# One fused VectorE instruction per modulation tile, one borrowed weight tile put back into the ring, and two branch hints

## The chip, the core and the metric

The kernel runs on one NeuronCore of one Trainium2 chip. The core has a matmul engine (TensorE, PE in the profile), three engines for elementwise work (VectorE or DVE, ScalarE or ACT, GpSimd or POOL), SyncE (SP), which here issues nearly all DMAs, and 16 DMA engines. PE reads SBUF and writes PSUM; a PSUM bank holds 128x512 f32 values. Each engine works through its own list of instructions in order and meets the others at semaphores. The metric is device time in microseconds, lower is better.

## The reference

One layer of a diffusion backbone over 512 latent tokens and 256 context tokens of width 1024. The conditioning vector `c` gives six rows of modulation (shift, scale and gate for each half of the layer):

```
sh1, sc1, gt1, sh2, sc2, gt2 = split(silu(c) @ ada_w + ada_b, 6)
h   = rms_norm(x, norm1_g) * (1 + sc1) + sh1
...   one projection of h; two branches (retention, long convolution), merged by sigmoid gates, w_out -> mix
x   = x + gt1 * mix
h2  = rms_norm(x, norm2_g) * (1 + sc2) + sh2
x   = x + gt2 * moe(h2)
out = rms_norm(x, final_norm_g)
```

The mixture of experts picks one of 4 groups per token and 2 of its 8 experts; each expert is (silu(u w1) * (u w3)) w2 with a hidden width of 512. Rows 1 and 2 of the modulation (`sh1`, `sc1`) are needed at the start; the later four (`gt1`, `sh2`, `sc2`, `gt2`) only after the merge of the branches.

## The kernel before

**Order.** Up to the merge, Tile's scheduler places the instructions of each engine from the program order and priorities; `weave` interleaves a bulk stream of matmuls with side work, one step of each in turn. The start and the last stages are ordered by hand. In the expert stage PE alone is in hand order (`tensor_order`), and a `no_sync_barrier` is a line that the scheduler moves nothing across; it costs no instruction.

**The merge stage.** `fm_group` (through `stream`) multiplies a weight by activations held as pairs of a high and a low part (three matmuls, `mm3`, lines 201 to 203). A weight arrives as `raw` (two k-blocks per load, two buffers); ACT rounds the high part `wH` (line 197), DVE subtracts it for the low part `wL` (line 198), three buffers each. Four PSUM banks collect a group's result; the next group needs them back. Groups `gr` and `gh` are evacuated by ACT (sigmoid), `ho` and `ro` by DVE (lines 1121, 1125, 1126). They run in the order gr, gh, ho, ro, gr, gh, ho, ro for two halves of the channels.

**The later modulation rows.** From the first `ho` on the generator `rest_of_modulation` is woven in. `ada_sums` (line 333 on) computes two rows of the modulation at a time without PE: for each of 8 k-blocks and both rows it loads a 128x1024 tile of `ada2` (SP, line 340, into `ring`, four buffers of tag "c"), scales it by the per-partition value silu(c) on DVE (line 341), and, but for the first, adds it to `acc` on POOL (line 343). That is 32 tiles in two calls, 28 of them added. `ada_rows` sums `acc` over the partitions on PE (line 349), `to_columns` transposes the rows (line 357), `columns` adds the bias on DVE (line 361), and a small product `lc` of PE (line 1081) uses the result at once.

**The expert stage.** 16 pairs of experts, 12 weight tiles of 1 MB per pair: tiles 12a to 12a+7 for `up` (lines 1497), 12a+8 to 12a+11 for `down` (line 1522); pairs 2g and 2g+1 make group g. `ahead(n)` lets SP issue loads up to tile n in a fixed order. Most go to `ring_`, 10 buffers of 1 MB (tag "ew", line 1224). `loans` lists the tiles that borrow other buffers instead: two of every 13 borrow the four halves of `xm` (line 1206), one of every 13 the buffers xe0 and xe1. Tiles 128 to 131 are taken out of the `xm` loans, since the branch below uses `xm`.

**The overflow branch.** A pass gives each expert 64 token places. If an expert has more tokens, further rounds are needed: `overflow()`, called in group 5 (a = OV = 10), loads the number of rounds into a register of every engine, and `tc.If(rounds > 1)` (line 1560) skips or enters a loop nest that loads weights into the `xm` buffers. In the profiled run it is skipped. Ahead of it SP has issued up to tile 131 (`ahead(12 * OV + 8 + OA)`, OA = 4), and PE ends with `add(parts, places[4:])` (`co` matmuls, line 1537).

Of the kernel before, what the change touches and what calls it, by code (L numbers as in the profile page):

```python
# [15 lines left out]
ALU = mybir.AluOpType  # L16
# [12 lines left out]
GENERAL = True  # L29
OV = 10  # L30
OA = 4
NA, NB, NC, NR, NW, NH = 12, 33, 4, 10, 2, 3
# [141 lines left out]
def body(es: ExitStack, tc: tile.TileContext, d, out, dump=None):  # L174
    nc = tc.nc
    V, A, T, G, S = nc.vector, nc.scalar, nc.tensor, nc.gpsimd, nc.sync
# [13 lines left out]
    def bank(name, tag="x"):  # L190
        return ps.tile([128, 512], F32, name=name, tag=tag, bufs=4)
# [39 lines left out]
    def wide(name, shape=(128, 1024), dt=F32):  # L231
        return pa.tile(list(shape), dt, name=name, tag="a", bufs=NA)

    def ring(name, shape=(128, 1024), dt=F32):
        return pb.tile(list(shape), dt, name=name, tag="c", bufs=NC)
# [43 lines left out]
    scT = sm.tile([128, 8, 32], F32, name="scT")  # L279
# [54 lines left out]
    def ada_sums(r, acc):  # L334
        for k in range(8):
            for i in range(2):
                if k == 0:
                    acc.append(wide("acc"))
                w = ring("adaw")
                tc.keep_in_program_order(S.dma_start(w, d["ada2"][2 * r - 2 + i, :, k, :]))  # L340
                V.tensor_scalar(out=w if k else acc[i], in0=w, scalar1=scT[:, k, 0:1], scalar2=None, op0=ALU.mult)
                if k:
                    G.tensor_tensor(out=acc[i], in0=acc[i], in1=w, op=ALU.add)  # L343
                yield

    def ada_rows(acc, rows):
# [834 lines left out]
    def borrow(pool, tag, bufs, units):  # L1181
        def tile_():
            w = pool().tile([128, units, 512], F32, name="xw" + tag, tag=tag, bufs=bufs)
            return [w[:, u] for u in range(units)], w.rearrange("p a b -> p (a b)")
        return tile_
# [6 lines left out]
    early_tiles = len(sequence)  # L1192
    sequence += range(early_tiles, len(plan))

    loans.update((i, lent_xm) for i in range(early_tiles, len(plan) - 4)
                 if (i - early_tiles) % (NR + 3) < 2 and not 12 * OV + 8 <= i < 12 * OV + 8 + OA)
    loans.update((i, [borrow(wk_, "xe0", 1, 2), borrow(lambda: late, "xe1", 1, 2)]) for i in range(early_tiles, len(plan) - 4)
                 if (i - early_tiles) % (NR + 3) == XE)
    ready, lent = {}, {}
# [2 lines left out]
    def borrowed(src, places):  # L1202
        units = []
        for u, w in places:
            c0 = 512 * len(units)
            S.dma_start(w, src(slice(c0, c0 + 512 * len(u))))
            units += u
        return units

    def ahead(n):  # L1210

        while issued[0] < min(n, len(plan)):
            i = sequence[issued[0]]
            src = plan[i]
            issued[0] += 1
            if i in loans:
                if i < early_tiles and not lent:

                    lent.update((j, [place() for place in loans[j]]) for j in AL)
                ready[i] = borrowed(lambda c: src[:, c], lent.pop(i, None) or [place() for place in loans[i]])  # L1220
                continue
            w = ring_.tile([128, 2048], F32, name="ew", tag="ew")
            if i < len(plan) - 4:
                S.dma_start(w, src)  # L1224
            else:
                wv = w.rearrange("p (a b) -> p a b", a=4)
                for h in ((0, 4),) if i < len(plan) - 1 else ((0, 2), (2, 4)):
                    S.dma_start(wv[:, h[0]:h[1]], src[:, h[0]:h[1]])
            ready[i] = [w[:, 512 * u:512 * u + 512] for u in range(4)]
# [166 lines left out]
    for t in range(1, 4):  # L1396
# [6 lines left out]
                           op0=ALU.add, op1=ALU.mult)  # L1403
# [102 lines left out]
    def turned(hh):  # L1506
        p = bank("hT")
        for q in range(4):
            T.transpose(p[:, 128 * q:128 * q + 128], hh[:, 128 * q:128 * q + 128], ident)  # L1509
        hT_ = wk.tile([128, 512], F32, name="hT", tag="hT", bufs=2)  # L1510
        V.tensor_copy(hT_, p)
        return hT_
# [27 lines left out]
    def add(parts, places):  # L1540
        for t, n in places:
            ns = slice(512 * n, 512 * n + 512)
            p = bank("co")
            combine(parts, t, n, p, True)
            V.tensor_tensor(out=xmid[:, t, ns], in0=xmid[:, t, ns], in1=p, op=ALU.add)  # L1545
# [10 lines left out]
    def overflow():  # L1556
        later = wk.tile([128, CAP], F32, name="later")
        V.tensor_copy(later, slots)
        rounds = nc.values_load(nrounds[0:1, 0:1], min_val=0, max_val=8)
        with tc.If(rounds > 1):  # L1560
            with tc.For_i(1, rounds, 1):
                V.tensor_scalar(out=later, in0=later, scalar1=float(CAP), scalar2=None, op0=ALU.add)
                with tc.For_i(0, 16, 1) as pi:
                    pos2 = wk.tile([128, 4, 2], F32, name="pos2", tag="fs")
                    V.tensor_copy(pos2, pos[:, :, bass.ds(pi * 2, 2)])
                    whl2 = wk.tile([128, 4, 4], F32R, name="whl2", tag="whl2")
                    V.tensor_copy(whl2, f(wHL[:, :, bass.ds(pi, 1)].rearrange("p t a h e -> p t (a h e)")))
                    sel = []
                    run(select_steps(pos2, 2, "x", sel, later, "y", 4))
                    gt, xg = sel  # L1570

                    def weights(stage, kc, i, e):
                        t_, k1 = (d["w2"], 1) if stage else (d[("w1", "w3")[i]], 2)
                        return borrowed(lambda c: t_[bass.ds(pi * 2 + e, 1), :, 2 * k1 * kc + k1 * c.start // 1024:
                                                     2 * k1 * kc + k1 * c.stop // 1024, :]
                                        .rearrange("o p a b -> p (o a b)"), [place() for place in lent_xm])

                    cmb, wsl = spread(gt, 0, whl2)
                    ab_ = [bank("ga", "acc"), bank("up", "acc")]
                    for kc in range(2):  # L1580
                        up_half(ab_, kc, xg, 0, weights)
                    add([(cmb, down(turned(hidden(ab_)), wsl, weights))], places)
# [12 lines left out]
    more = chosen(0, sel)  # L1595
# [31 lines left out]
    parts = []  # L1627
    for g in range(8):
        a = 2 * g
        ahead(early_tiles + XE if g == 0 else 12 * OV + 8 + OA if a == OV else 12 * a + early_tiles + 14)  # L1630
        if g == 0:
            ab_ = [bank("ga", "acc"), bank("up", "acc")]
            up_half(ab_, 0, sel[1], 0, ahead_weights)
            run(more)
            shares()
            t1e.close()
            late = es.enter_context(tc.tile_pool(name="late", bufs=1, side="right", reuse_waits="tile"))
            ahead(early_tiles + 14)
            up_half(ab_, 1, sel[1], 0, ahead_weights)
            hh = hidden(ab_)  # L1640
            spr = [spread(sel[0], 128 * j, weights_of(j)) for j in range(2)]
            hT_ = turned(hh)
        else:
            hh = up(a, sel[1])
            add(parts, places[:4])
            hT_ = turned(hh)
            add(parts, places[4:])
        parts = []
        if a == OV and GENERAL:
            region.__exit__(None, None, None)  # L1650
            tc.no_sync_barrier()
            overflow()
            region = tensor_order()
            region.__enter__()
        ahead(12 * a + early_tiles + 20)
        now, nxt = spr, []
        parts.append((now[0][0], down(hT_, now[0][1], ahead_weights)))
        more = chosen(g + 1, nxt) if g < 7 else iter(())
        some(more, 1)
        if g == 7:  # L1660
            fn = wk.tile([128, 1024], F32, name="fn", tag="gt", bufs=1)
            for j in range(2):
                row = wk.tile([1, 512], F32, name="fr%d" % j, tag="cmb", bufs=4)
                S.dma_start(row, d["fnorm"][:, 512 * j:512 * j + 512])
                G.partition_broadcast(fn[:, 512 * j:512 * j + 512], row)
        hh = up(a + 1, sel[1])
        if g < 7:
            some(more, 3)
            hT_ = turned(hh)
            run(more)  # L1670
            spr = [spread(nxt[0], 128 * j, weights_of(a + 2 + j)) for j in range(2)]
            parts.append((now[1][0], down(hT_, now[1][1], ahead_weights)))
            sel = nxt
# [74 lines left out]
    with tc.manual_schedule():  # L1748
        ys_ = [bank("y", "acc"), bank("y", "x")]
        w = [[ahead_weights(1, n, 0, e) for e in range(2)] for n in range(2)]  # L1750
# [43 lines left out]
```

## Time and profile before

| | |
|---|---|
| median of 3 runs | 1158.91 us (1158.83 to 1163.09) |
| the profiled execution | 1160.5 us, its span 1158.5 us |
| PE busy in the span | 1109.2 us |
| DVE busy | 616.3 us |
| ACT busy | 349.8 us |
| POOL busy | 92.8 us |
| DMA moved | 283.22 MB, 244 GB/s over the span |

Times in the profile count from the start of the span. In its rows, the engine stands before the line of the kernel, the operation and the tiles (written <- read), then shapes and the count. `x4 | 5.1, 1284 | 0.3 <- ...` means four instructions, busy 5.1 us, 1284 ns each on the mean, and 0.3 us in which the engine stood idle before them, with what ended the idle time. `A <- B: 6.2, 1, 6.2` in the view of waits: A waited for B 6.2 us in total, once, 6.2 us at the longest. A `q` behind an engine (SPq, PEq) is its sequencer: waits, branches, DMA issues. PE's rows overlap, as matmuls are pipelined; the step from one start to the next is the better measure.

### The profile page before, as it was taken

How to read it: one execution, taken by the hardware profiler on the slowest of the kernel's cores; microseconds unless marked ns; L12 is line 12 of the kernel's file. 1: busy time of each engine (PE TensorE's matmuls, PEld its weight loads, DVE VectorE, ACT ScalarE, POOL GpSimd, SP SyncE). 2: the span in 40 equal slices, each digit the busy share in tenths (PEclk: the TensorE clock that was granted, in tenths of full speed). 3: DMA queues.
4: the chain of work that ended last, by engine and by line, in shares of the span. 5: the costliest groups of instructions: out<-in, count | busy, mean ns of one | idle time of the engine just before them, and what ended most of it. 6: DMA issues, size and time to landing. Idle time of an engine off the chain costs nothing. (4 is left out here: it accounts for less than half of the span.)

```text
span 1158.5 us, 13777 instructions
## 1 busy us (share of the span) xinstructions
PE 1109.2 (96%) x5338; PEld 714.9 (62%) x5338; DVE 616.3 (53%) x1041; ACT 349.8 (30%) x620; POOL 92.8 (8%) x69
## 2 busy tenths in 40 slices
PE   6999999999999997779999999999999999899996
PEld 3667888877778776558775735454545454444543
DVE  1778996675466759988543623333333333232234
ACT  2486352445444463223243411020202020101112
POOL 0010000000000005676000000000000000000000
PEclk8999999999999998889999999999999999999998
DMA  7653343121222045565384888999999994999992
GB/s 263 196 176 102 113 142 125 55 73 55 73 73 73 19 156 192 179 218 182 109 332 195 320 324 345 417 419 418 415 417 416 419 416 173 418 418 417 418 406 102
DMA packets 63279, 283.22 MB, mean 244 GB/s; under 512 B 6822, under 2 KB 8998, under 8 KB 44778
## 3 DMA queue, kind: packets, MB, share of 16 engines
q1 hardware_dynamic: 61114, 274.51, 62.2%
q0 software_dynamic: 2096, 7.80, 2.1%
q8 instruction: 43, 0.70, 0.2%
q14 instruction: 26, 0.21, 0.0%
HBM read 280.18 MB, written 2.10 MB: 244 GB/s over the span
## 5 line engine op out<-in xcount | busy, mean ns | idle before, releaser
L198 DVE TENSOR_TENSOR wL<-raw,wH 128x512 fp32r<-128x512 f32 x142 | 131.3, 931 | 118.1 <-ACT wH L197 110.0
L197 ACT CAST wH<-raw 128x512 fp32r<-128x512 f32 x142 | 88.1, 621 | 232.0 <-PE ro L202 34.9
L1497 PE MATMUL ga<-ew,xgm 128*64 128x512 f32 x408 | 110.3, 593 | 2.2 <-DMA ew<-w 2.2
L1503 DVE TENSOR_TENSOR hh<-hh,up 128x512 f32<-128x512 f32 x16 | 11.0, 688 | 184.5 <-PE up L1497 184.5
L1497 PE MATMUL up<-ew,xgm 128*64 128x512 f32 x376 | 103.3, 593 | 2.7 <-DMA ew<-w 2.7
L1522 PE MATMUL y<-ew,hT 128*64 128x512 f32 x368 | 95.9, 595 | 2.9 <-PEq L1560 1.9
L343 POOL TENSOR_TENSOR acc<-acc,adaw 128x1024 f32<-128x1024 f32 x28 | 74.3, 2664 | 84.6 <-PE gh L202 43.7
L197 ACT CAST yh<-yv 128x512 fp32r<-128x512 f32 x30 | 18.5, 618 | 200.1 <-DVE yv L1528 188.5
L1497 PEld LDWEIGHTS ga<-ew,xgm 128*64 128x64 f32 x408 | 34.1, 137 | 61.4 <-issue 53.7
L1497 PEld LDWEIGHTS up<-ew,xgm 128*64 128x64 f32 x376 | 32.9, 137 | 55.3 <-issue 47.6
L1465 PE MATMUL xg<-gtm,h2H 128*128 128x256 f32 x256 | 60.5, 280 | 0.0
L1466 PE MATMUL xg<-gtm,h2L 128*128 128x256 f32 x256 | 59.8, 278 | 0.0
L1522 PEld LDWEIGHTS y<-ew,hT 128*64 128x64 f32 x368 | 29.8, 137 | 48.1 <-issue 44.4
L1528 DVE SCALAR_TENSOR_TENSOR yv<-y,wsl,gt 128x512 f32<-128x512 f32 x30 | 22.4, 748 | 61.6 <-PE y L1522 53.1
L1502 ACT ACTIVATE hh<-ga 128x512 f32<-128x512 f32 x16 | 9.6, 597 | 138.2 <-PE ga L1497 135.9
L1465 PEld LDWEIGHTS xg<-gtm,h2H 128*128 128x128 f32 x256 | 48.1, 188 | 0.8 <-issue 0.8
L1466 PEld LDWEIGHTS xg<-gtm,h2L 128*128 128x128 f32 x256 | 48.1, 188 | 0.0
L1545 DVE TENSOR_TENSOR xmid<-xmid,co 128x512 f32<-128x512 f32 x58 | 39.8, 688 | 12.5 <-PE co L1537 11.9
L1537 PE MATMUL co<-yh,cmb 128*128 128x512 f32 x114 | 46.1, 404 | 0.0
L1468 DVE TENSOR_TENSOR xgm<-xg,rss 128x256 f32<-128x256 f32 x64 | 27.0, 424 | 35.3 <-PE xg L1466 35.3
L1537 PE MATMUL co<-yl,cmb 128*128 128x512 f32 x114 | 44.7, 392 | 0.0
L1469 ACT ACTIVATE xgm<-xgm,sh2c 128x256 f32<-128x256 f32 x64 | 32.4, 509 | 35.7 <-DVE xgm L1468 35.7
(479 smaller groups left out, 2437.0 us busy)
## 6 DMA issues: line engine op xcount, KB each, us to landing
ew<-w SPq DMA_DIRECT2D x147, 1024.0 KB, 13.6
xwxm<-w SPq DMA_DIRECT2D x54, 512.0 KB, 15.0
raw<-w_in SPq DMA_DIRECT2D x52, 512.0 KB, 3.7
adaw<-ada SPq DMA_DIRECT2D x32, 512.0 KB, 5.2
xwxe<-w SPq DMA_DIRECT2D x26, 512.0 KB, 17.4
adaw<-ada SPq DMA_DIRECT2D x32, 256.0 KB, 5.9
raw<-ret_w_o SPq DMA_DIRECT2D x8, 512.0 KB, 3.7
raw<-w_out SPq DMA_DIRECT2D x8, 512.0 KB, 4.0
```

The costliest lines, as they stand in the source:

```text
L197: A.copy(h, src)
L198: V.tensor_tensor(out=l, in0=src, in1=f(h), op=ALU.subtract)
L343: G.tensor_tensor(out=acc[i], in0=acc[i], in1=w, op=ALU.add)
L1465: T.matmul(p, h2[0][:, t, ks], gt[:, t], start=(t == 0), stop=False)
L1466: T.matmul(p, h2[1][:, t, ks], gt[:, t], start=False, stop=(t == 3))
L1468: V.tensor_tensor(out=x_, in0=p, in1=rss, op=ALU.mult)
L1469: A.activation(x_, x_, AF.Identity, bias=sh2c[:, k:k + 1])
L1497: T.matmul(ab_[i][64 * e:64 * e + 64], xg[k][:, c0 + 64 * e:c0 + 64 * e + 64], w[e][q], start=(k == 0), stop=(k == 7))
L1522: T.matmul(y_[n][64 * e:64 * e + 64], hT_[:, 128 * k + 64 * e:128 * k + 64 * e + 64], w[e][2 * q + n], start=(k == 0), stop=(k == 3))
L1528: V.scalar_tensor_tensor(out=yv, in0=y_[n], scalar=wsl, in1=gt2[:, ns], op0=ALU.mult, op1=ALU.mult)
L1537: T.matmul(p, cmb[:, 128 * t:128 * t + 128], y[j][:, ns], start=(start and i + j == 0), stop=(i == len(parts) - 1 and j == 1))
L1545: V.tensor_tensor(out=xmid[:, t, ns], in0=xmid[:, t, ns], in1=p, op=ALU.add)
```

## The change

Three edits. In `ada_sums` the scaling on DVE and the addition on POOL become one `scalar_tensor_tensor` on DVE (tile times scalar plus `acc`) for the 28 tiles that are added; the first tile of each sum keeps its scaling. In `loans` the range that is left out of the `xm` loans grows by 8 tiles, from 128..131 to 128..139; a tile in it that was to borrow `xm` uses the ring. The branch gets a label, and two hint instructions (`LikelyTaken`) for it are placed: on SP ahead of the loads of tiles 128 to 131, and on PE between the two halves of the `co` matmuls ahead of the branch, each between two scheduling barriers.

```
@@ ada_sums
-                V.tensor_scalar(out=w if k else acc[i], in0=w, scalar1=scT[:, k, 0:1], scalar2=None, op0=ALU.mult)
                 if k:
-                    G.tensor_tensor(out=acc[i], in0=acc[i], in1=w, op=ALU.add)
+                    V.scalar_tensor_tensor(out=acc[i], in0=w, scalar=scT[:, k, 0:1], in1=acc[i], op0=ALU.mult, op1=ALU.add)
+                else:
+                    V.tensor_scalar(out=acc[i], in0=w, scalar1=scT[:, k, 0:1], scalar2=None, op0=ALU.mult)
@@ loans
-                 if (i - early_tiles) % (NR + 3) < 2 and not 12 * OV + 8 <= i < 12 * OV + 8 + OA)
+                 if (i - early_tiles) % (NR + 3) < 2 and not 12 * OV + 8 <= i < 12 * OV + 8 + OA + 8)
@@ overflow
-        with tc.If(rounds > 1):
+        with tc.If(rounds > 1, label="more"):
@@ the loop over groups, a = 2 * g
+        if a == OV and GENERAL:
+            ahead(12 * OV + 8)
+            tc.no_sync_barrier()
+            tc.mark_branch_hint_location("more", hint="LikelyTaken", engines=[mybir.EngineType.SP])
+            tc.no_sync_barrier()
         ahead(early_tiles + XE if g == 0 else 12 * OV + 8 + OA if a == OV else 12 * a + early_tiles + 14)
...
             hT_ = turned(hh)
+            if a == OV and GENERAL:
+                tc.no_sync_barrier()
+                tc.mark_branch_hint_location("more", hint="LikelyTaken", engines=[mybir.EngineType.PE])
+                tc.no_sync_barrier()
             add(parts, places[4:])
```

Here `early_tiles` is 14, `NR` 10 and `GENERAL` true.

## The prediction

> **What bounds the kernel now.** I read the page first (busy time, slices), then the waits of PE, then the stretches in which PE waits, engine by engine. TensorE (PE) is busy through nearly the whole span, so time can come only from the few places where it waits or runs slowly.
>
> ```profile
> PE 1109.2 (96%) x5338; PEld 714.9 (62%) x5338; DVE 616.3 (53%) x1041; ACT 349.8 (30%) x620; POOL 92.8 (8%) x69
> ...
> PEclk8999999999999998889999999999999999999998
> ```
>
> The granted clock dips in slices 15 to 17 of 40 (434 to 521 us). This is the merge stage, where the later modulation rows are summed between matmuls. The waits of PE from 433.5 to 576.2 us, and the stretches in which the clock is halved (columns: stretch, its length, then busy us and count of PE, PEld, DVE, ACT, POOL, clock, DMA share, GB/s):
>
> ```profile
> PE lc L1081 <- DVE sh2c L361: 6.9, 1, 6.9
> PE ro L201 <- DVE sig L1121: 6.2, 1, 6.2
> PE gr L201 <- DVE sig L1125: 5.0, 1, 5.0
> PE ro L203 <- DVE wL L198: 1.0, 1, 1.0
> ```
> ```profile
> 449.00:455.84 6.84, 4.54 (x11) 3.65 (x12) 6.41 (x9) 0.00 (x0) 1.53 (x2) 0.50 0.62 210
> ...
> 479.73:486.56 6.83, 4.05 (x10) 3.22 (x11) 6.83 (x10) 1.50 (x3) 1.48 (x1) 0.50 0.67 222
> ...
> 513.87:520.69 6.82, 4.04 (x23) 3.29 (x23) 4.24 (x5) 0.00 (x0) 5.93 (x3) 0.50 0.37 139
> ```
>
> All four waits are for VectorE (DVE): 19.1 us. Behind each of the three long ones the clock is 0.50, and PE works 4.54, 4.05 and 4.04 us in that state; half of it is lost, 6.3 us. So 25.4 us hang on DVE being late. Why it is late:
>
> ```profile
> 433.50:550.00 116.50, 97.38 (x406) 75.43 (x406) 104.39 (x90) 34.13 (x56) 74.47 (x29) 0.91 0.58 194
> ```
> ```profile
> L198 DVE TENSOR_TENSOR wL<-raw,wH 128x512 fp32r<-128x512 f32 x32 | 56.1, 1766 | 6.8 <-ACT wH L197 6.8
> L341 DVE TENSOR_SCALAR adaw<-adaw,scT 128x1024 f32<-128x1024 f32 x27 | 30.5, 1149 | 2.1 <-DMA adaw<-ada 2.1
> ...
> L198 DVE TENSOR_TENSOR retL<-o,retH 128x512 fp32r<-128x512 f32 x8 | 7.6, 956 | 0.0
> ```
> ```profile
> L198 DVE TENSOR_TENSOR wL<-raw,wH x32: 677/1687/2884, 434.2 to 550.0; 128x512 fp32r<-128x512 f32 x32
> ...
> L341 DVE TENSOR_SCALAR adaw<-adaw,scT x28: 735/743/2891, 432.7 to 543.0; 128x1024 f32<-128x1024 f32 x28
> ...
> L343 POOL TENSOR_TENSOR acc<-acc,adaw x28: 2376/2713/2842, 433.6 to 546.0; 128x1024 f32<-128x1024 f32 x28
> ```
>
> DVE is busy 104.4 of 116.5 us, 90%. But the same wL instruction takes 0.68 us or 2.9, and the scaling of one tile 0.74 or 2.9. The timelines of GpSimd (POOL) and DVE show when:
>
> ```profile
> 475.72 5.50 POOL L343 TENSOR_TENSOR acc<-acc,adaw 128x1024 f32<-128x1024 f32 x2 [1.36 <-DVE adaw L341]
> ```
> ```profile
> 476.16 5.60 DVE L198 TENSOR_TENSOR wL<-raw,wH 128x512 fp32r<-128x512 f32 x2
> 481.68 1.27 DVE L1125 TENSOR_TENSOR sig<-sig,ro 128x512 f32<-128x512 f32 x2
> ```
>
> Two wL that lie inside two POOL additions last as long as these (5.60 against 5.50 us). L1125, for whose PSUM bank PE waits 5.0 us, stands behind them. Much of what is counted as DVE work here is waiting for POOL.
>
> The second place is the overflow branch at 960 to 1100 us. Its rows: the first `co` matmul of the expert groups 4 to 7, then what line 1560 (the branch) did, then the issues of SP, then the DMA rate in 2 us slices from 930 us.
>
> ```profile
> 907.79 0.50 PE L1537 MATMUL co<-yh,cmb 128*128 128x512 f32 x1
> ...
> 967.84 0.50 PE L1537 MATMUL co<-yh,cmb 128*128 128x512 f32 x1
> ...
> 1035.21 0.50 PE L1537 MATMUL co<-yh,cmb 128*128 128x512 f32 x1
> ...
> 1097.85 0.50 PE L1537 MATMUL co<-yh,cmb 128*128 128x512 f32 x1
> ```
> ```profile
> L1560 SPq EVENT_SEMAPHORE  x8: 17/17/17, 965.2 to 965.8; - x8
> ...
> L1560 SPq COMPARE_BRANCH  x1: 50/50/50, 958.6 to 958.6; - x1
> ...
> L1560 PEldq COMPARE_BRANCH  x1: 3618/3618/3618, 973.8 to 973.8; - x1
> ```
> ```profile
> 937.48 20.48 SPq L1224 DMA_DIRECT2D ew<-w  x5
> 977.51 0.87 SPq L1206 DMA_DIRECT2D xwxm<-w  x2
> 978.43 3.64 SPq L1224 DMA_DIRECT2D ew<-w  x6
> ```
> ```profile
> GB/s 404 434 408 422 418 414 430 422 408 412 426 430 401 422 389 414 164 16 0 0 0 0 8 4 174 365 354 418 410 442 414 426 410 414 412 420 438 410 422 408
> ```
>
> A group of four experts takes 60.05 us up to the branch (967.84 - 907.79), then 67.37, then 62.64: 7.32 + 2.59 = 9.9 us over. SP issues nothing from 958 to 977.5, so the DMA engines run dry at 964 and are at full rate again after 980. The load of tile 132 (`xwxm`) stands first, and six ring loads follow it at once: they had only stood behind it.
>
> ```profile
> SPq L1206 <- PEq L1560: 11.3, 1, 11.3
> ```
> ```profile
> 977.76 7.09 PE L1522 MATMUL y<-ew,hT 128*64 128x512 f32 x32 [1.86 <-PEq L1560]
> ```
>
> SP waited 11.3 us there for PE's passing of the branch, and PE itself lost 1.9 us at it (the bracket of its next row).
>
> **The modulation sums.** Removed: 28 scalings on DVE (27 of them in the row: 30.5 us) and 28 additions on POOL (2.71 us each, about 74 us). Added: 28 scalar_tensor_tensor of 128x1024 with two SBUF sources on DVE. The trace has none of that width. Nearest rows:
>
> ```profile
> L517 DVE SCALAR_TENSOR_TENSOR cv<-up,pp,cv x24: 743/746/751, 78.2 to 152.3; 128x511 f32<-128x511 f32 x24
> ```
> ```profile
> L411 DVE SCALAR_TENSOR_TENSOR fsd<-win,l x8: 1131/1151/1173, 74.5 to 93.3; 128x512 f32<-128x512 f32 x8
> ```
> ```profile
> L1545 DVE TENSOR_TENSOR xmid<-xmid,co 128x512 f32<-128x512 f32 x58 | 39.8, 688 | 12.5 <-PE co L1537 11.9
> L1468 DVE TENSOR_TENSOR xgm<-xg,rss 128x256 f32<-128x256 f32 x64 | 27.0, 424 | 35.3 <-PE xg L1466 35.3
> ```
>
> 256 more columns cost 0.264 us, so L517's 0.746 becomes 0.746 + 2 x 0.264 = 1.27 us at 1024. Lower bound: 0.74, the scaling it replaces. Upper bound: twice L411, which writes its halves interleaved, 2.30. I take 1.27, from L517, which has the same contiguous form with two SBUF sources and a per-partition scalar: 28 x (1.27 - 0.74) = 14.8 us more DVE work.
>
> With POOL quiet the stretched instructions fall to their minima: wL 56.1 - 32 x 0.68 = 34.3, retL 7.6 - 8 x 0.68 = 2.2, the scalings 30.5 - 27 x 0.74 = 10.5; together 47 us. DVE then has 104.4 - 47 + 14.8 = 72 us to do, in a stretch that would shrink by 22 us to 94: 77%. It keeps up on the whole, with little to spare at the transitions, where the evacuations of four banks and the splits come together. So I leave an estimate at each: 0.7 us at `ho` to `ro`, one wL that stands ahead; 1 us at `ro` to `gr`, one evacuation (1.27 us for two in the row of L1125) and the hand-over; 1.5 us at `lc`, where two small additions and a wL between them must pass after the transposes. That is 3.2 of 19.1 us, none long enough for the clock: it halved behind waits of 5.0 us and more and not behind 1.0. Gain: 15.9 + 6.3 = 22.2 us.
>
> The loads are an SP matter: an `adaw` buffer comes free at the end of the DVE instruction instead of POOL's, which takes away SP's waits for POOL here, and lets the next weight loads pass earlier.
>
> ```profile
> SPq L340 <- POOL acc L343: 10.5, 5, 2.8
> ```
> ```profile
> DMA to landing us min/median/max: 3.8/5.5/7.8
> ```
>
> **Tile 132 and the hints.** The longer exclusion takes in only one more borrowed tile, 132: the others of 128 to 139 are ring tiles, or 139, which another line lends. Tile 132 now takes the ring buffer of 121, 133 to 137 those of 122 to 125 and 127, 138 that of 128. PE's reading of 120 onwards:
>
> ```profile
> 954.00 3.60 PE L1497 MATMUL ga<-ew,xgm 128*64 128x512 f32 x16
> 957.44 3.60 PE L1497 MATMUL up<-ew,xgm 128*64 128x512 f32 x16
> ```
>
> Two tiles go per 3.43 us, so 132 may go at once after the branch, 133 and 134 at 961, 135 and 136 at 964.5, 137 at 968. None waits for the branch on PE. At 2.5 us per tile (1.05 MB at 418 GB/s) they keep the DMA busy to about 980, where 128 comes free. So of the dry 15 us some 2 to 3 remain (1 to 2 more if SP still stalls from 958.6 to 965.2 at its own branch). Tiles 138 and 139 land near 987; PE reads them about 993. There is 6 us to spare, and the following group, which before lost 2.6, starts with loads ahead. I cost the lost ring buffer at nothing for that reason; if the cover went, it would be one tile, 2.5 us. DMA waits gone: 9.9 - 1.9 = 8.0 us.
>
> The hint on PE, some 30 matmuls ahead of the branch, should hide the 3.6 us that the branch takes: 1.5 of PE's 1.9 us. Bounds: 0 if it does nothing, 3.6 us lost if what it fetches displaces PE's own next instructions. [...] The scheduling barriers order nothing that DVE or ACT lack time for there.
>
> **Sum.** 22.2 + 8.0 + 1.5 = 31.7 us. On the profiled execution (1160.5 us, span 1158.5) that gives 1128.8; the median of the runs is 1158.9, 1.6 lower, so I forecast 1127.
>
> **The rivals.**
> *DVE becomes the bound.* The new instruction costs 2.30 us, as L411's row would have it: 28 x (2.30 - 1.27) = 29 us more than I count, DVE 101 us where PE needs 94; these 7 us go, and some 4 more where DVE is late at the transitions (half the clock's 6.3 and 1 us of waits): 1127 + 11 = 1138. For it: L411 also has two SBUF sources. Against it: L517 has too, at 0.746. [...] 10%.
> *The ring is no release.* The wait of SP for PE's branch moves to tile 133, or the exclusion changes nothing that decides: then only the merge stage gains, 1158.9 - 22 = 1137. For it: every engine meets at line 1560. Against it: six ring loads went out in 3.64 us, unhindered. 10%.
> *Slower: the DVE queue stands behind its own loads.* A fused instruction waits for its load in order, ahead of the wL that PE needs. A load takes up to 7.8 us; POOL's slowness has given it time. It decides if each of the 16 pairs of loads holds DVE over 2.3 us beyond what the three weight buffers cover (16 x 2.3 = 37, more than all that can be won). At 3 us each: 48 - 32 = 16 us slower, 1175. Against it: DVE waited 2.1 us in all for these loads, and SP gets rid of 10.5 us of waits. 4%.
> *It does nothing that counts* (a new order of the instructions takes back what is won): 1157. 3%.
>
> **How the numbers follow.** Forecast 73%. The best case, no wait left at all, is 1158.9 - 25.4 - 9.9 = 1123.6; with the scatter of the runs I begin at 1120. The upper end takes in the two rivals that lose one of the halves, 1138, and a little more: 1141. Outside stay some 10%. Faster by over 0.5% (5.8 us, about what a measurement of this kernel can tell from no change): 73 + 10 + 10, and 1 of the rest, 0.94; same 0.02; slower 0.04.
>
> **What would show it.** In the merge stage: wL at 0.68 us throughout, the fused instruction near 1.27, clock 1.0 from 434 to 576 us, PE's waits for DVE under 4 us in all. At the branch: tile 132 issued before 966 us of today's count, no run of zeros in the DMA rate, groups of 60 us on both sides, PE's branch well under 3.6 us. A fused instruction of 2 us or more, DVE waiting for `adaw`, or SP still silent until PE has passed the branch would make it wrong.

## The result, and the profile after

| | before | after |
|---|---|---|
| median | 1161.0 us (4 runs, 1158.8 to 1164.1) | 1124.6 us (4 runs, 1124.1 to 1125.2) |
| the profiled execution, its span | 1160.5, 1158.5 us | 1124.3, 1122.6 us |

The ratio is 0.9685, 95% interval [0.9656, 0.9713]: 36.6 us less than before by this ratio. 1127.0 us was forecast. (The runs of before beside the kernel after have a median 2 us above the 1158.9 that the forecast starts from.)

The page of the kernel after: busy time and the granted clock.

```profile
PE 1100.6 (98%) x5338; PEld 710.5 (63%) x5338; DVE 582.1 (52%) x1041; ACT 349.4 (31%) x620; POOL 18.6 (2%) x41
...
PEclk8999999999999999999999999999999999999999
```

The three dips of the clock in slices 15 to 17 are gone, and POOL has 28 instructions fewer. The waits of PE from 433.5 to 1110 us are down to two:

```profile
PE y L1523 <- DVE hT L1512: 1.1, 1, 1.1
PE y L1523 <- PEq L1561: 0.5, 1, 0.5
```

The merge stage of the kernel after: the stretch of 96.5 us (busy us and count of PE, PEld, DVE, ACT, POOL, then clock, DMA share, GB/s), then the fused instruction and the split wL on DVE, and DVE's waits.

```profile
433.50:530.00 96.50, 96.50 (x432) 76.36 (x431) 72.42 (x95) 33.05 (x56) 0.18 (x1) 1.00 0.72 239
```
```profile
L342 DVE SCALAR_TENSOR_TENSOR acc<-adaw,scT,acc x28: 1277/1283/1286, 430.6 to 514.3; 128x1024 f32<-128x1024 f32 x28
```
```profile
L198 DVE TENSOR_TENSOR wL<-raw,wH x45: 682/691/693, 431.8 to 559.6; 128x512 fp32r<-128x512 f32 x45
```
```profile
DVE acc L342 <- DMA adaw<-ada: 9.9, 7, 2.1
```

PE is busy in all 96.5 us at full clock. DVE is busy 72.4 of them (75%), and every wL takes 0.69 us where it took up to 2.88. DVE now waits 9.9 us for the weight loads, which it did for 2.1 us before, but no wait of PE follows from it.

The branch after: the first `co` matmul of groups 4 to 7, then the branch (now line 1561), the two hints, and the DMA rate in 2 us slices from 900 us.

```profile
881.10 0.50 PE L1538 MATMUL co<-yh,cmb 128*128 128x512 f32 x1
...
941.14 0.50 PE L1538 MATMUL co<-yh,cmb 128*128 128x512 f32 x1
...
1002.01 0.50 PE L1538 MATMUL co<-yh,cmb 128*128 128x512 f32 x1
...
1062.04 0.50 PE L1538 MATMUL co<-yh,cmb 128*128 128x512 f32 x1
```
```profile
L1561 SPq EVENT_SEMAPHORE  x8: 17/17/17, 938.0 to 940.5; - x8
L1561 SPq COMPARE_BRANCH  x1: 70/70/70, 932.6 to 932.6; - x1
...
L1561 PEldq COMPARE_BRANCH  x1: 2341/2341/2341, 947.1 to 947.1; - x1
```
```profile
L1801 SPq BRANCH_PREFETCH_HINT  x1: 56/56/56, 924.4 to 924.4; - x1
L1801 PEldq BRANCH_PREFETCH_HINT  x1: 45/45/45, 943.1 to 943.1; - x1
```
```profile
GB/s 414 412 424 416 418 418 418 418 434 403 408 432 416 418 418 393 344 410 406 53 66 279 426 430 414 434 406 303 383 317 393 410 434 418 438 389 414 420 420 426
```

The groups take 60.04, 60.87 and 60.03 us: 0.8 us over instead of 9.9. The dry stretch of the DMA engines has shrunk to two slices. SP is still silent at its branch, though its hint came 8.2 us earlier: the branch is at 932.6, the first instruction behind it at 938.0, the next load at 940.6. PE's branch takes 2.3 us and ends 6.3 us after PE's hint.

Matched matmul by matmul, PE is 2.3 us ahead of before already at its hundredth matmul (33.3 against 31.0 us), when the first stretch at half clock was shorter in that execution (6.8 us instead of 10.2): this is no work of the change. From the first `ho` to the first `wo` matmul, 142.7 us become 116.8: 25.8 us. Then 1.6 us are given back in expert group 0, where the clock is halved behind the 1.1 us wait for hT (which the kernel before has too, at full clock):

```profile
647.38:650.79 3.41, 3.41 (x10) 0.99 (x10) 1.10 (x4) 0.00 (x0) 0.00 (x0) 0.50 0.46 186
```

At the branch 9.1 us are gained. 2.3 + 25.8 - 1.6 + 9.1 = 35.6 of the 35.9 us between the spans.

### The profile page after: what moved, and what is told of

Same layout as the page of the kernel before. It is cut to its first block, busy times and chain, and to the rows that moved or that the text cites. A ratio compares the mean times of both kernels' runs of the same rounds, so it can differ in the third digit from the quotient of the medians.

```text
span 1122.6 us, 13708 instructions
## 1 busy us (share of the span) xinstructions
PE 1100.6 (98%) x5338; PEld 710.5 (63%) x5338; DVE 582.1 (52%) x1041; ACT 349.4 (31%) x620; POOL 18.6 (2%) x41
## 5 line engine op out<-in xcount | busy, mean ns | idle before, releaser
L198 DVE TENSOR_TENSOR wL<-raw,wH 128x512 fp32r<-128x512 f32 x142 | 97.2, 688 | 120.0 <-ACT wH L197 111.3
L1498 PE MATMUL up<-ew,xgm 128*64 128x512 f32 x376 | 100.9, 592 | 0.0
L1498 PEld LDWEIGHTS up<-ew,xgm 128*64 128x64 f32 x376 | 31.9, 137 | 54.3 <-issue 52.9
L342 DVE SCALAR_TENSOR_TENSOR acc<-adaw,scT,acc 128x1024 f32<-128x1024 f32 x28 | 35.6, 1282 | 10.8 <-DMA adaw<-ada 10.7
```

The costliest lines, as they stand in the source:

```text
L198: V.tensor_tensor(out=l, in0=src, in1=f(h), op=ALU.subtract)
L342: V.scalar_tensor_tensor(out=acc[i], in0=w, scalar=scT[:, k, 0:1], in1=acc[i], op0=ALU.mult, op1=ALU.add)
L1498: T.matmul(ab_[i][64 * e:64 * e + 64], xg[k][:, c0 + 64 * e:c0 + 64 * e + 64], w[e][q], start=(k == 0), stop=(k == 7))
```

## The experiments

Two questions. In the merge stage: is it POOL's quiet that helps, as argued, or that there is one instruction instead of two? At the branch: what do the ring and the two hints do, each for itself? The theory is that of the prediction (POOL's additions stretched what DVE did at the same time; tile 132 held up the loads behind it; the hints are worth little); the rivals stand in each expectation. The median of before beside these kernels was 1161.3 to 1162.0 us.

**The fused instruction alone** (the first hunk of the diff, nothing else).

> The kernel before with the fused VectorE instruction alone; ring range and branch as before. Theory (the merge stage's delay came from POOL's additions holding up DVE, and the half clock behind it): the merge stage shortens by about 25 us as in the kernel after, PE waits for nothing in it, the branch still costs its 9 to 10 us; some 1135 us, ratio about 0.978. Rival (the ring and the hints carry the gain, the merge stage pays only in part): 1145 us or more. The new 1.1 us wait of PE in expert group 0 and the half clock behind it should be there already, if the earlier arrival at that place causes it; if the ring or the hints cause it, it is not.

Measured: 1134.8 us, ratio 0.9783 [0.9768, 0.9798], 25 us less. No wait of PE in the merge stage; first `ho` to first `wo` 116.8 us as in the kernel after. The two groups at the branch still take 8.7 us too much. So the merge stage's part stands by itself. Group 0's wait of 1.1 us is there, the half clock behind it isn't.

**The POOL load put back.**

```
                 if k:
                     V.scalar_tensor_tensor(out=acc[i], in0=w, scalar=scT[:, k, 0:1], in1=acc[i], op0=ALU.mult, op1=ALU.add)
+                    G.tensor_tensor(out=w, in0=w, in1=w, op=ALU.add)
```

> The kernel after, with one more POOL addition of 128x1024 behind each fused instruction (the tile added to itself; nothing reads the result), so that VectorE has the work of the kernel after and POOL is as busy as in the kernel before. Theory (what stretched VectorE's instructions was POOL's work at the same time): the split wL takes up to 2.9 us again, the merge stage gets back PE's waits and the half clock, 15 to 25 us slower than the kernel after, 1140 to 1150 us. Rival (the gain comes from there being fewer or shorter VectorE instructions, POOL is of no account): wL stays at 0.68 us, 1125 us, within 2 us of the kernel after.

Measured: 1152.5 us, ratio 0.9923 [0.9900, 0.9947], 28 us above the kernel after. PE's waits from 380 to 1110 us, and the longest stretch at half clock, in this kernel:

```profile
PE gr L201 <- DVE sig L1127: 6.7, 1, 6.7
PE lc L1083 <- DVE sh2c L363: 6.1, 1, 6.1
PE ro L201 <- DVE sig L1123: 5.2, 1, 5.2
PE ro L203 <- DVE wL L198: 1.1, 2, 0.7
```
```profile
475.20:485.44 10.24, 5.50 (x13) 4.37 (x14) 10.24 (x13) 1.94 (x4) 3.45 (x2) 0.50 0.59 206
```
```profile
L342 DVE SCALAR_TENSOR_TENSOR acc<-adaw,scT,acc x28: 1269/1274/2916, 429.8 to 542.4; 128x1024 f32<-128x1024 f32 x28
```

The three waits are back with their 18.0 us in the places that they had before, and the clock is halved behind each. DVE executes what it executes in the kernel after; only POOL is busy beside it (50.1 of the 96.5 us from 433.5 us on, 0.2 in the kernel after), and single instructions of 1.27 us now last 2.9. The wL take 1.38 us on the mean instead of 0.69, at most 2.4 where 2.9 was expected:

```profile
L198 DVE TENSOR_TENSOR wL<-raw,wH 128x512 fp32r<-128x512 f32 x32 | 43.9, 1381 | 8.2 <-ACT wH L197 7.8 <-PE ho L202 0.2
```

POOL also holds each `adaw` buffer longer here, but late loads are not the reason: DVE waited 2.3 us for them, against 9.9 in the kernel after. The time is 2.5 us above the range expected. The clock was halved for 27 us here, for 20.5 before, which may account for it.

**Two DVE instructions, POOL quiet.**

```
+                V.tensor_scalar(out=w if k else acc[i], in0=w, scalar1=scT[:, k, 0:1], scalar2=None, op0=ALU.mult)
                 if k:
-                    V.scalar_tensor_tensor(out=acc[i], in0=w, scalar=scT[:, k, 0:1], in1=acc[i], op0=ALU.mult, op1=ALU.add)
-                else:
-                    V.tensor_scalar(out=acc[i], in0=w, scalar1=scT[:, k, 0:1], scalar2=None, op0=ALU.mult)
+                    V.tensor_tensor(out=acc[i], in0=acc[i], in1=w, op=ALU.add)
```

> The kernel after, with the fused instruction split into two on VectorE (scale at 0.74 us, add at 1.3 to 1.4 us), POOL quiet. Theory: POOL's quiet gives most of the gain; VectorE has some 0.8 x 28 = 22 us more to do in the merge stage, 94 of 96.5 us, so it just about keeps up, with some waits of PE at the transitions: 1126 to 1136 us. Rival (the fusing itself carries the gain): 1150 us or more. Rival (VectorE has room that its busy time hides): 1125 us, no wait in the stage.

Measured: 1124.9 us, ratio 0.9675 [0.9653, 0.9696]: the time of the kernel after. Its first 96.5 us of the merge stage, and the addition:

```profile
433.50:530.00 96.50, 95.08 (x425) 74.90 (x424) 89.64 (x124) 35.85 (x59) 0.18 (x1) 1.00 0.74 248
```
```profile
L343 DVE TENSOR_TENSOR acc<-acc,adaw x28: 1207/1218/1226, 436.7 to 526.1; 128x1024 f32<-128x1024 f32 x28
```

DVE is busy 89.6 of 96.5 us (93%), and PE waits for it once, 1.4 us at `lc`. So the fusing saves 0.68 us an instruction (0.75 + 1.22 against 1.28), of which next to nothing reaches the time. What counted is that POOL adds nothing any more (busy 0.2 of the 96.5 us). More waits had been expected (1126 to 1136 us); the rival that VectorE has room that its busy time hides came nearest. DVE kept up here at 93% with every wL under 0.70 us; in the kernel before, at 90% with wL of up to 2.88 us, it did not.

**The ring alone** (the second hunk).

> The kernel before with the longer exclusion alone (tile 132 loads into a ring buffer); no hints, modulation as before. Theory (tile 132 stood at the branch and held up every load behind it): PE's waits for loads behind the branch go, its own wait at the branch (1.9 us) stays or grows a little since instruction fetch now meets full DMA traffic; 8 us less, some 1151 to 1153 us, ratio 0.993. Rival 1 (the wait only moves to tile 133): no change, 1159 to 1161. Rival 2 (it is the hints that bring the branch's gain): under 4 us less.

Measured: 1158.6 us, ratio 0.9978 [0.9965, 0.9990]: 2.6 us, a third of what was expected. The waits for loads behind the branch are all gone, as the theory has it. But PE's branch itself has become longer:

```profile
PE y L1522 <- PEq L1560: 4.8, 1, 4.8
```
```profile
L1560 PEldq COMPARE_BRANCH  x1: 6585/6585/6585, 974.3 to 974.3; - x1
```

Before, PE passed its branch in 3.6 us while the DMA rate stood at 0 to 8 GB/s. Here, with the loads running at 418 to 430 GB/s, it takes 6.6; PE waits 4.8 us instead of 1.9, and the clock is halved behind it for 6.8 us. The ring took one wait away and made the other one longer.

While PE passes its branch in the kernel before (973.8 to 977.4 us), a single DMA packet moves, 16 KB on the queue q8, of the kind "instruction":

```profile
DMA packets 1, 0.02 MB, mean 5 GB/s; under 512 B 0, under 2 KB 0, under 8 KB 0
q8 instruction: 1, 0.02, 2.1%
```

It starts 1.0 us after the branch and lasts 1.2, and the branch ends 1.4 us behind it. With the ring the packet starts only 4.1 us after the branch, beside the loads; it lasts 1.1, and the branch again ends 1.4 us behind it. So the branch's 3.0 us more go with the 3.1 us by which this packet starts later. In all eleven profiles in which PE's branch takes 2 us or more, it ends 1.4 us behind the end of a q8 packet; so q8 is read as the queue of PE's instructions.

**The hints alone** (the last three hunks).

> The kernel before with the two hints alone. Theory: PE's wait at the branch falls from 1.9 us to about 0.5, but tile 132 still stands behind PE's passing of the branch, the DMA queues run dry as before and PE waits for the loads; a gain of 0 to 2 us, no measurable change, some 1157 to 1160 us. If PE passes the branch earlier by 1.5 us, tile 132 goes out earlier by as much, which may add 1.5 us of gain. Rival (the hints release SP): the DMA's dry stretch goes, 8 us less.

Measured: 1156.4 us, ratio 0.9962 [0.9948, 0.9976]: 4.4 us, more than expected. PE's branch is down to 0.5 us and its wait to 0.3:

```profile
L1560 PEldq COMPARE_BRANCH  x1: 485/485/485, 975.4 to 975.4; - x1
```

The q8 packet starts 1.1 us after the hint and is over before the branch. The DMA queues still run dry, from 967 to 979 us, so SP is not released. Besides, one ring load more stands ahead of SP's branch than before (issued at 960.6, SP's branch at 961.0): the scheduling barriers have changed SP's order, which the expectation did not count. What this load gave of the 4.4 us, the runs do not show.

**After without the hints, in two ways**: without both hints and their barriers; and without SP's hint and its barriers but with PE's barriers left in place, so that SP issues its loads in the order of the kernel after:

```
             if a == OV and GENERAL:
                 tc.no_sync_barrier()
-                tc.mark_branch_hint_location("more", hint="LikelyTaken", engines=[mybir.EngineType.PE])
-                tc.no_sync_barrier()
             add(parts, places[4:])
```

> The kernel after without the two hints (fused instruction and ring stay). Theory (the hint on SP hides nothing, the one on PE part of the branch): PE's branch takes 3.6 us or more and PE waits about 1.5 to 3 us there instead of 0.5; 1 to 2.5 us slower than the kernel after, some 1126 us. SP's silence at the branch is as long as with the hint (about 6 us) or 2 us shorter, since nothing of it was hidden. Rival (the hints are worth nothing): the same as after within 0.5 us, PE's wait at the branch 0.5 us. Rival (the hints carry the branch's gain): 1130 us or more, with waits of PE for loads.

> The kernel after without either hint, but with SP's loads in its order (one ring load more ahead of SP's branch than in the kernel without hints, which ran 1131.1 us). Theory (PE's fetch of the code behind the branch takes 6.6 us when the DMA queues are full, and the hint on PE hides it): PE's branch takes 6 us or more, PE waits nearly 5 us there and the clock is halved behind it, some 1130 to 1131 us. Rival (it is the order of SP's loads that made the kernel with hints faster): 1125 us, PE's wait at the branch under 1 us.

Measured: 1131.1 us, ratio 0.9733 [0.9720, 0.9746], 5 us above what was expected, and 1130.0 us, ratio 0.9720 [0.9702, 0.9739], as expected. PE waits for no load in either. PE's branch takes 6.7 and 5.9 us, its wait is 4.8 and 4.1. In the first of the two, the wait and the half clock behind it:

```profile
954.70 1.12 PE L1523 MATMUL y<-ew,hT 128*64 128x512 f32 x2 [4.84 <-PEq L1561]
```
```profile
951.80:958.63 6.83, 3.93 (x10) 1.37 (x12) 1.43 (x4) 0.00 (x0) 0.00 (x0) 0.50 0.63 252
```

4.8 us of wait and half of 3.93 us of work at half clock make 6.8, and the group takes 67.0 us instead of 60.05. So with SP's loads in the same order the hints account for 4 to 5.5 us (1130.0 against 1126.0 without SP's hint, below, and 1124.6 in the kernel after). What the order of SP's loads gives is not shown: 1.1 us lie between the two medians, and their intervals overlap.

**After without SP's hint.**

```
-            tc.mark_branch_hint_location("more", hint="LikelyTaken", engines=[mybir.EngineType.SP])
```

(and the `ahead` and the two barriers around it).

> The kernel after without the hint on SP (the hint on PE stays, and SP issues its loads in the same order). Theory (SP's hint hides nothing): SP is silent for as long as with it or up to 2 us shorter, PE's branch and waits as in the kernel after; the same time within 1 us. Rival (SP's hint saves what SP would wait for): SP silent for 2 us or more longer, and 1 us or more slower.

Measured: 1126.0 us, ratio 0.9693 [0.9674, 0.9712], not told apart from the kernel after. SP issues nothing for 8.3 us (933.4 to 941.8) against 8.0 with its hint (932.6 to 940.6): the hint hides nothing there. In all kernels with the ring this silence lasts 8.0 to 8.9 us with SP's hint and 6.7 to 9.1 without. PE's branch takes 2.1 us as before. The one difference is that PE now waits until VectorE has passed the branch:

```profile
PE y L1523 <- DVEq L1561: 1.4, 1, 1.4
```

That is 0.9 us more than the kernel after loses, and the two groups take 1.6 us too much instead of 0.8. The other kernel with PE's hint and without SP's, further below, has the same wait, and no profile with both hints has it. Why the first `y` matmul then waits for VectorE as well, the runs do not show.

**PE's hint 16 matmuls earlier**, beside SP's hint; without SP's hint; and without it but with 16 more warming matmul calls in group 0 (the last hunk below, in that kernel alone). The kernel after was timed again beside the first and the last of the three.

```
             hh = up(a, sel[1])
+            if a == OV and GENERAL:
+                tc.no_sync_barrier()
+                tc.mark_branch_hint_location("more", hint="LikelyTaken", engines=[mybir.EngineType.PE])
+                tc.no_sync_barrier()
             add(parts, places[:4])
             hT_ = turned(hh)
-            if a == OV and GENERAL:
-                tc.no_sync_barrier()
-                tc.mark_branch_hint_location("more", hint="LikelyTaken", engines=[mybir.EngineType.PE])
-                tc.no_sync_barrier()
...
             hT_ = turned(hh)
+            keep_warm(8)
         else:
```

> The kernel after with the hint on PE four output tiles (16 matmuls, 3.7 us) earlier. Theory (the fetch takes some 6 us from the hint under full DMA traffic, so the hint of the kernel after comes 2 us too late): PE's branch shrinks from 2.3 us to under 0.6, and PE's wait at the branch is gone or what VectorE's own passing of the branch leaves of it; 0 to 0.7 us less, not measurable in the time, seen in the branch's own duration. Rival (2.1 to 2.3 us are what a hinted branch costs however early): the branch stays at 2.1 to 2.3 us.

> The kernel after with the hint on PE as much earlier, no hint on SP, and 16 short warming matmuls in expert group 0 where PE waits 1.1 us for VectorE's hT copy. Theory: the 1.1 us wait stays a wait in the sum (the warming matmuls fill it and shorten nothing), but no half clock can follow it; 0 to 2.5 us less than the kernel after, some 1122 to 1125 us. Rival (the warming matmuls run longer than the wait): 0.5 to 1 us slower.

> The kernel after itself, run beside the last two on the same chip: 1124.6 us as first timed, between 1123.5 and 1126.5. Theory on the half clock in expert group 0, which the first profile of this kernel showed and the profiles without the hints did not: it comes by chance behind the 1.1 us wait, so this profile may be without it. Rival (it belongs to this kernel): it is there again.

> The kernel after with the hint on PE 16 matmuls earlier and no hint on SP: the last but one kernel without its warming matmuls. With the earlier hint PE's branch took 0.4 us beside SP's hint and 6.1 us in the kernel that had no hint on SP and the warming matmuls ahead. Theory (what a hint fetched can be gone again by the time of the branch, depending on where PE's instructions lie, which the warming matmuls shifted): the branch takes under 0.6 us here, 1124 to 1126 us. Rival (SP's hint is what keeps PE's early hint useful): the branch takes 6 us again, 1130 us.

Measured: 1124.9 us, ratio 0.9679 [0.9660, 0.9698]; 1132.8, 0.9754 [0.9737, 0.9772]; the kernel after again 1124.0, 0.9687 [0.9664, 0.9709]; and without SP's hint 1127.4, 0.9705 [0.9688, 0.9722]. PE's branch with the early hint, first beside SP's hint, then with the warming matmuls:

```profile
L1561 PEldq COMPARE_BRANCH  x1: 397/397/397, 947.4 to 947.4; - x1
```
```profile
L1561 PEldq COMPARE_BRANCH  x1: 6125/6125/6125, 949.9 to 949.9; - x1
```

With the hint 10.3 us ahead PE's branch takes 0.4 us, here and in the kernel without SP's hint. With the warming matmuls in group 0 it takes 6.1 us, though the hint stands as far ahead of the branch: SP's hint was not the cause, since the kernel that differs only by the warming matmuls has 0.4 us again. That what the hint fetched was gone again, as the last expectation has it, is not what the trace shows. Between hint and branch there is one packet on q8 in the first of these kernels and none in the kernel with the warming matmuls (a packet on q14 stands there in the kernels without a hint too):

```profile
q8 instruction: 1, 0.02, 0.6%
q14 instruction: 1, 0.01, 0.2%
```
```profile
q14 instruction: 1, 0.01, 0.2%
```

There the q8 packet starts 3.6 us after the branch, and 3.4 to 4.2 us after it in the three kernels with full queues and no hint on PE: the hint brought no packet. The q8 packet ahead of the hint came 25.1 us before the branch, and 20.1 to 20.7 us in the other kernels. Whether the one has to do with the other, the runs do not show.

The matmuls also ran 2.4 us longer than the wait that they were to fill. The half clock in group 0 is absent in the second profile of the kernel after, and present in that without SP's hint (1127.4 us, above the 1124 to 1126 expected): it comes and goes behind a wait that all these kernels but the one with the warming matmuls have. None of the kernels is faster than the kernel after.

The branch in all kernels (DMA: the rate while PE passes it; "packet": when the q8 packet starts, counted from PE's hint or, without one, from PE's branch; "over": what the two groups around it take beyond 2 x 60.05 us):

| kernel | DMA | hint on PE | packet, us | PE's branch, us | PE's wait there, us | over, us |
|---|---|---|---|---|---|---|
| before | dry | none | 1.0 | 3.6 | 1.9 | 9.9 |
| fused alone | dry | none | 1.0 | 3.3 | 1.5 | 8.7 |
| ring alone | full | none | 4.1 | 6.6 | 4.8 | 7.6 |
| after without hints | full | none | 4.2 | 6.7 | 4.8 | 7.0 |
| the same, SP's order kept | full | none | 3.4 | 5.9 | 4.1 | 6.0 |
| hints alone | dry | 3.9 us ahead | 1.1 | 0.5 | 0.3 | 5.3 |
| after, two profiles | full | 3.9, 4.0 us ahead | 3.9, 3.6 | 2.3, 2.1 | 0.5, 0.3 | 0.8, 0.5 |
| POOL load put back | full | 3.9 us ahead | 3.7 | 2.2 | 0.4 | 0.8 |
| two DVE instructions | full | 3.9 us ahead | 4.4 | 2.8 | 1.0 | 1.3 |
| after without SP's hint | full | 3.9 us ahead | 3.6 | 2.1 | 1.4 | 1.6 |
| hint earlier | full | 10.3 us ahead | 2.1 | 0.4 | 0.3 | 0.8 |
| hint earlier, no SP hint | full | 10.3 us ahead | 2.1 | 0.4 | 1.4 | 1.6 |
| the same, warming matmuls | full | 10.3 us ahead | none; 3.6 from the branch | 6.1 | 4.3 | 6.2 |

## Why the prediction held, point by point

**The merge stage: right, by its mechanism, and 3.6 us too small.** 22.2 us were counted, 25.8 came. The fused instruction was taken at 1.27 us and took 1.283; wL and retL fell to 0.69 us; DVE's 72 us came to 72.4. Of the 3.2 us that were left at the transitions nothing was to be seen; even with DVE at 93% PE waited only 1.4. The rival at 2.30 us, which went by L411's row, is out. The two SBUF sources that spoke for it cost L517 nothing in the kernel before: with them it took 0.746 us at 511 columns, and the same instruction with one of its two sources in PSUM took 0.748 us at 512:

```profile
L1528 DVE SCALAR_TENSOR_TENSOR yv<-y,wsl,gt 128x512 f32<-128x512 f32 x30 | 22.4, 748 | 61.6 <-PE y L1522 53.1
```

Against the scaling with its one source (0.75 us at 1024 columns), the fused instruction took 1.7 times as long (1.28 us).

**The slower rival's mechanism appeared, and was covered.** DVE's waits for its loads rose from 2.1 to 9.9 us, no longer than 2.1 us at once. With 24 us idle in the 96.5, this cost nothing.

**The branch: the sum right (9.5 against 9.1 us), its terms wrong.** The step that failed is the split into 8.0 us for tile 132 and 1.5 us for PE's hint, each counted for itself. PE's 3.6 us at the branch were taken as a fixed price, though the row stood beside a DMA rate of zero, and the very edit that fills the DMA again made 6.6 us of it: the q8 packet, 1.4 us behind whose end the branch ends, started 4.1 us after the branch instead of 1.0. The ring alone gave 2.6 us, the hints alone 4.4; the ring with the hints on top of the fused instruction gave some 10 (1134.8 to 1124.6). Given the ring, the hints are worth 4 to 5.5 us, not 1.5.

**SP's hint did not shorten SP's stall, as one clause feared** ("1 to 2 more if SP still stalls"): SP was silent for 8 us. The cover held: tiles 138 and 139 came in time, and PE waited for no load. The rival that the ring is no release named the wrong cause: the loads were released, and of the 8.0 us counted for them 2.6 came by the ring alone and 3.7 on top of the fused instruction (1134.8 to 1131.1).

**By luck:** 2.3 us of the profiled execution are the clock at the start, and 1.6 us the other way are the half clock in group 0. Neither belongs to the change. And the forecast starts from 1158.9 us, where the median of before beside the kernel after is 1161.0: the gain was forecast at 31.9 us and came to 36.4 between the medians, so the forecast time lies nearer to the measured one than the forecast gain does.

## What to carry to other kernels

When one engine's short instructions last now 0.7 and now 2.9 us, look which other engine is busy at those moments before counting the first as loaded: here taking the work off GpSimd was worth 25 us, and saving VectorE an instruction nothing. A stall measured while the DMA queues are dry need not be the stall that remains once they are full: here PE's branch took 3.6 us, then 6.6. Where an edit fills the queues, ask what else goes through them. Two edits at one place are tried one by one and together: here they gave 2.6 and 4.4 us alone, and 9 to 10 together.

## What was not expected of the hardware

- PE's branch, which skips the loop nest, took 3.3 to 3.6 us with dry DMA queues and 5.9 to 6.7 us with full ones (five kernels without a hint on PE). In all five it ended 1.4 us behind the end of a 16 KB packet on the queue q8, which started 1.0 us after the branch with dry queues, 3.4 to 4.2 us with full ones. The page of the kernel after has these packets among its DMA queues:

```profile
q8 instruction: 43, 0.70, 0.3%
q14 instruction: 26, 0.21, 0.1%
```

- With a hint on PE this packet started 1.1 to 4.4 us after the hint, in all kernels but one. The branch took 0.4 us with 10.3 us of lead, 0.5 us with 3.9 us and dry queues, 2.1 to 2.8 us with 4 us and full queues, where it ended 6.1 to 6.8 us after the hint. In the kernel with the warming matmuls no q8 packet started between hint and branch, and the branch took 6.1 us in spite of 10.3 us of lead. On SP the hint shortened SP's silence in no run (8.0 to 8.9 us with it and the ring, 6.7 to 9.1 without); that PE waited for VectorE in the two kernels with PE's hint and without SP's (1.4 us in both) is unexplained.
- Within the stages spoken of here, the clock was halved (0.50) behind every wait of PE of 4.1 us and more; behind the wait of 1.1 us in group 0 it was in three of the thirteen profiles that have it (the kernel after in one of two, the hints alone, the early hint without SP's).
